# The tail of a relu-and-mean kernel: another cut of the last row, a third partial sum, and another order of the last three waits

## The chip, the cores and the metric

The kernel runs on one core of a Trainium2 chip. The metric is device time in microseconds (us), lower is better. A span is the time of one profiled execution as its trace has it; it is about 1.3 us shorter than the device time of the same run.

## The reference

```python
x: (32, 512, 1024) float32
return np.mean(np.maximum(x, 0), axis=-1)      # (32, 512) float32
```

That is 16384 rows of 1024 numbers: 67.1 MB in, 64 KB out, and one pass of cheap arithmetic.

## The kernel before

All rows are streamed from HBM (the memory that holds x) into SBUF (the memory that the engines compute from) by DMA loads that SyncE issues. Two compute engines, ScalarE and VectorE, take the rows by turns, each with one instruction that applies the maximum with 0 and adds up along the row. The loads grow smaller toward the end (16 rows a partition, then 6, 4, 2, 1), and the last row of each partition comes in three pieces of columns, so that little work is left after the last byte. Each load and each engine raises a semaphore, a counter that others wait for; an engine's count below is the update that says that its piece of the last row is done. In the code P is 128 partitions and D 1024 columns, and the comments are added for this text.

```python
col_pieces = [512, 256, 256]
...
last = sbuf("last", P, D + 2)            # the last row, and 2 columns for partial sums
scale = sbuf("scale", P, D // 4 + 2)     # 1/1024 everywhere
...
nc.scalar.wait_ge(loaded[i + 1], 16)     # first piece
act_row(nc, last[:, :512], last[:, D:D + 1]).then_inc(act, 1)
nc.vector.wait_ge(loaded[i + 2], 16)     # second piece
dve_row(nc, last[:, 512:768], last[:, D + 1:D + 2]).then_inc(dve, 1)
nc.vector.wait_ge(act, n_done + 1)       # ScalarE's count: its partial sum is there
nc.vector.wait_ge(dve, n_done + 1)       # VectorE's own count: its own partial sum is there
nc.vector.wait_ge(loaded[i + 3], 16)     # third piece
nc.vector.scalar_tensor_tensor(          # the last instruction: third piece and both partial sums
    out=last[:, 768:], in0=last[:, 768:], scalar=0.0, in1=scale[:, :],
    op0=ALU.max, op1=ALU.mult, accum_out=res[:, J - 1:J],
).then_inc(dve, 1)
... # SyncE waits for it and stores res
```

The last instruction reads 256 columns and the two partial sums behind them in one go. The source makes it wait for three things. In the program as it is built, each compute instruction carries at most one wait. The one that the source writes first goes on the instruction itself, and the two others go on one EventSemaphore instruction ahead of it (called the wait instruction from here on). So here the wait instruction carries the load and the own count, and the last instruction itself waits for ScalarE's count.

Of the kernel before, what the change touches and what calls it, by code (L numbers as in the profile page):

```python
# [12 lines left out]
def act_row(nc, src, acc):  # L13

    return nc.scalar.activation(out=src, in_=src, func=ACT.Relu, accum_out=acc)  # L15


def dve_row(nc, src, acc, init=None):

    return nc.vector.tensor_scalar(  # L20
        out=src, in0=src, scalar1=0.0, scalar2=init,
        op0=ALU.max, op1=ALU.add, accum_out=acc,
    )
# [22 lines left out]
def kernel(  # L46
# [10 lines left out]
    nc = tc.nc  # L57
    P = nc.NUM_PARTITIONS
    xf = x.flatten_outer_dims()
    R, D = xf.shape  # L60
# [13 lines left out]

    row_pieces = [6, 4, 2, 1]
    assert full * NB + sum(row_pieces) + 1 == J
    col_pieces = [512, 256, 256]
    assert sum(col_pieces) == D

    def sbuf(name, *shape):  # L80
        return ctx.enter_context(nc.sbuf_tensor(name, list(shape), F32))
# [2 lines left out]
    sums, res, part = sbuf("sums", P, J), sbuf("res", P, J), sbuf("part", P, 2)  # L84


    last = sbuf("last", P, D + 2)
    scale = sbuf("scale", P, D // 4 + 2)

    row0, mean0, turned0 = sbuf("row0", P, 2, D), sbuf("mean0", P, 32), sbuf("turned0", P, 32)  # L90

# [1 line left out]
    loaded = [nc.alloc_semaphore(f"loaded{i}") for i in range(full + len(row_pieces) + len(col_pieces) + 2)]  # L93
    act, dve, pool = (nc.alloc_semaphore(n) for n in ("act", "dve", "pool"))
# [38 lines left out]
    lo, i = 0, full  # L133
    for n in row_pieces:
        load(i, xt[:, lo:lo + n, :], xr[:, j0 + lo:j0 + lo + n, :])
        lo, i = lo + n, i + 1
    c = 0
    for w in col_pieces:
        load(i, last[:, c:c + w], xr[:, J - 1, c:c + w])
        c, i = c + w, i + 1  # L140
# [37 lines left out]
    lo, i = 0, full  # L178
    for n in row_pieces[:-1]:
        rows(i, xt, lo, n, j0)  # L180
        lo, i = lo + n, i + 1
# [12 lines left out]
        out=res[:, J - 2:J - 1], in0=part[:, 0:1], scalar1=part[:, 1:2], scalar2=inv, op0=ALU.add, op1=ALU.mult,  # L194
    ).then_inc(pool, 1)
    nc.scalar.wait_ge(loaded[i + 1], 16)
    act_row(nc, last[:, :512], last[:, D:D + 1]).then_inc(act, 1)
    nc.vector.wait_ge(loaded[i + 2], 16)
    dve_row(nc, last[:, 512:768], last[:, D + 1:D + 2]).then_inc(dve, 1)
    nc.vector.wait_ge(act, n_done + 1)  # L200
    nc.vector.wait_ge(dve, n_done + 1)
    nc.vector.wait_ge(loaded[i + 3], 16)
    nc.vector.scalar_tensor_tensor(  # L203
        out=last[:, 768:], in0=last[:, 768:], scalar=0.0, in1=scale[:, :], op0=ALU.max, op1=ALU.mult,
        accum_out=res[:, J - 1:J],
# [51 lines left out]
```

## Time and profile before

| | before |
|---|---|
| device time, median of 6 runs | 161.22 us (161.08 to 161.26) |
| span of the profiled run | 159.8 us |
| DMA queue, share of 16 engines' time | 97.8% |
| VectorE, ScalarE busy | 46%, 44% |
| last row's three pieces completely landed | 156.936, 157.298, 157.604 us |
| last VectorE instruction starts | 157.839 us |

The first four rows are read from the results and from the head of the page. The last two come from the trace's records of semaphore updates and instructions, which have single nanoseconds; the views round to 10 ns. The DMA engines carry the kernel and the compute engines wait for them (VectorE 84.6 us and ScalarE 83.8 us for main loads, by the view of waits). Only the two microseconds after the stream (157.604 to 159.795) are open to a change like this one. The prediction shows the lines.

### The profile page before, as it was taken

How to read it: one execution, taken by the hardware profiler on the slowest of the kernel's cores; microseconds unless marked ns; L12 is line 12 of the kernel's file. 1: busy time of each engine (PE TensorE's matmuls, PEld its weight loads, DVE VectorE, ACT ScalarE, POOL GpSimd, SP SyncE). 2: the span in 40 equal slices, each digit the busy share in tenths (PEclk: the TensorE clock that was granted, in tenths of full speed). 3: DMA queues.
4: the chain of work that ended last, by engine and by line, in shares of the span. 5: the costliest groups of instructions: out<-in, count | busy, mean ns of one | idle time of the engine just before them, and what ended most of it. 6: DMA issues, size and time to landing. Idle time of an engine off the chain costs nothing. (4 is left out here: it accounts for less than half of the span.)

```text
span 159.8 us, 350 instructions
## 1 busy us (share of the span) xinstructions
DVE 73.1 (46%) x131; ACT 70.3 (44%) x133; POOL 1.3 (1%) x9
## 2 busy tenths in 40 slices
DVE  0000029900499002990049800597007950089995
ACT  1400029800499002980049600595007930089974
POOL 1000000000000000000000000000000000000001
DMA  9969979899996997998979979969969969899993
GB/s 394 525 262 525 476 312 525 377 410 525 394 509 279 525 476 312 525 410 377 525 345 443 525 312 476 525 262 525 525 262 525 525 262 525 355 400 427 416 407 112
DMA packets 2608, 67.18 MB, mean 420 GB/s; under 512 B 560, under 2 KB 816, under 8 KB 1328
## 3 DMA queue, kind: packets, MB, share of 16 engines
q1 hardware_dynamic: 2608, 67.18, 97.8%
HBM read 67.11 MB, written 0.07 MB: 420 GB/s over the span
## 5 line engine op out<-in xcount | busy, mean ns | idle before, releaser
L20 DVE TENSOR_SCALAR_CACHE_REDUCE rows<-rows 128x1024 f32<-128x1024 f32 (+1 forms) x63 | 71.9, 1208 | 84.6 <-DMA rows<-in_x_dram 84.6
L15 ACT ACTIVATE rows<-rows 128x1024 f32<-128x1024 f32 (+1 forms) x63 | 65.2, 1035 | 83.9 <-DMA rows<-in_x_dram 83.8
L15 ACT ACTIVATION_READ_ACCUMULATOR rows<-rows 128x1 f32 x63 | 11.7, 186 | 0.0
L20 DVE DVE_READ_ACCUMULATOR rows<-rows 128x1 f32 x63 | 5.2, 82 | 0.0
L169 ACT ACT_TABLE_LOAD x1 | 1.3, 1283 | 3.5 <-DMA row<-in_x_dram 3.5
L169 ACT ACTIVATE row<-row 128x1024 f32<-128x1024 f32 x2 | 2.1, 1047 | 0.0
L159 POOL TENSOR_SCALAR res<-sums 128x112 f32<-128x112 f32 (+1 forms) x2 | 0.5, 244 | 153.9 <-DVE rows L20 153.9
L15 ACT ACTIVATE last<-last 128x512 f32<-128x512 f32 x1 | 0.6, 629 | 0.0
L20 DVE TENSOR_SCALAR_CACHE_REDUCE last<-last 128x256 f32<-128x256 f32 x1 | 0.4, 419 | 0.3 <-DMA last<-in_x_dram 0.3
L203 DVE SCALAR_TENSOR_TENSOR last<-last,scale 128x258 f32<-128x258 f32 x1 | 0.4, 428 | 0.1
L169 ACT ACTIVATION_READ_ACCUMULATOR row<-row 128x1 f32 x2 | 0.4, 186 | 0.0
L175 DVE STREAM_TRANSPOSE turned<-mean 128x32 f32<-128x32 f32 x1 | 0.2, 211 | 0.3 <-ACT row L169 0.3
L144 POOL MEMSET scale<- 128x258 f32 x1 | 0.3, 313 | 0.0
L193 POOL TENSOR_SCALAR res<-part 128x1 f32<-128x1 f32 x1 | 0.3, 264 | 0.5 <-DVE rows L20 0.5
L15 ACT ACTIVATION_READ_ACCUMULATOR last<-last 128x1 f32 x1 | 0.2, 186 | 0.0
L143 POOL MEMSET mean<- 128x32 f32 x1 | 0.1, 124 | 1.5 <-POOLq L55 1.5
L241 POOL MEMSET const-bfloat16-1.0<- 128x1 bf16 x1 | 0.1, 102 | 0.0
L241 POOL MEMSET const-uint8-127<- 128x1 uint8 x1 | 0.1, 102 | 0.0
L241 POOL MEMSET const-float32-0.0<- 128x1 f32 x1 | 0.1, 99 | 0.2 <-issue 0.2
L241 POOL MEMSET const-float32-1.0<- 128x1 f32 x1 | 0.1, 99 | 0.0
L203 DVE DVE_READ_ACCUMULATOR last<-last,scale 128x1 f32 x1 | 0.1, 85 | 0.0
L20 DVE DVE_READ_ACCUMULATOR last<-last 128x1 f32 x1 | 0.1, 82 | 0.0
## 6 DMA issues: line engine op xcount, KB each, us to landing
rows<-in_x_dram SPq DMA_DIRECT2D x1, 3072.0 KB, 36.7
rows<-in_x_dram SPq DMA_DIRECT2D x1, 2048.0 KB, 41.2
row<-in_x_dram SPq DMA_DIRECT2D x2, 512.0 KB, 22.3
rows<-in_x_dram SPq DMA_DIRECT2D x1, 1024.0 KB, 43.2
rows<-in_x_dram SPq DMA_DIRECT2D x1, 512.0 KB, 44.1
last<-in_x_dram SPq DMA_DIRECT2D x1, 256.0 KB, 44.3
last<-in_x_dram SPq DMA_DIRECT2D x2, 128.0 KB, 44.0
rows<-in_x_dram SPq DMA_DIRECT2D x7, 48.8
```

The lines of the kernel that those rows point to most:

```text
L15: return nc.scalar.activation(out=src, in_=src, func=ACT.Relu, accum_out=acc)
L20: return nc.vector.tensor_scalar(out=src, in0=src, scalar1=0.0, scalar2=init, op0=ALU.max, op1=ALU.add, accum_out=acc,)
L143: nc.gpsimd.memset(mean0[:, :], 0.0)
L144: nc.gpsimd.memset(scale[:, :], inv).then_inc(pool, 1)
L159: nc.gpsimd.tensor_scalar(out=res[:, lo:hi], in0=sums[:, lo:hi], scalar1=inv, scalar2=0.0, op0=ALU.mult, op1=ALU.add,).then_inc(pool, 1)
L169: done = nc.scalar.activation(out=row0[:, c, :], in_=row0[:, c, :], func=ACT.Relu, scale=inv, accum_out=mean0[:, c:c + 1],)
L175: nc.vector.transpose(turned0[:, :], mean0[:, :]).then_inc(first, 1)
L193: nc.gpsimd.tensor_scalar(out=res[:, J - 2:J - 1], in0=part[:, 0:1], scalar1=part[:, 1:2], scalar2=inv, op0=ALU.add, op1=ALU.mult,).then_i ...
L203: nc.vector.scalar_tensor_tensor(out=last[:, 768:], in0=last[:, 768:], scalar=0.0, in1=scale[:, :], op0=ALU.max, op1=ALU.mult, accum_out=r ...
L241: nc = _bacc.Bacc("TRN2", target_bir_lowering=False, num_devices=1)
```

## The change

The intent is to have less VectorE work after the last pieces land. The border between first and second piece moves from column 512 to 576. VectorE uses the time in which it is idle (0.29 us ahead of its piece in the trace of before) to take 128 columns of the first piece (a third partial sum), ScalarE keeps 448, and VectorE's second piece shrinks from 256 to 192 columns. The source also writes the load's wait ahead of the two counts, so that the last VectorE instruction itself waits for the last load.

```diff
-    col_pieces = [512, 256, 256]
+    col_pieces = [576, 192, 256]
...
-    last = sbuf("last", P, D + 2)
-    scale = sbuf("scale", P, D // 4 + 2)
+    last = sbuf("last", P, D + 3)
+    scale = sbuf("scale", P, D // 4 + 3)
...
     nc.scalar.wait_ge(loaded[i + 1], 16)
-    act_row(nc, last[:, :512], last[:, D:D + 1]).then_inc(act, 1)
+    act_row(nc, last[:, :448], last[:, D:D + 1]).then_inc(act, 1)
+    nc.vector.wait_ge(loaded[i + 1], 16)
+    dve_row(nc, last[:, 448:576], last[:, D + 1:D + 2])
     nc.vector.wait_ge(loaded[i + 2], 16)
-    dve_row(nc, last[:, 512:768], last[:, D + 1:D + 2]).then_inc(dve, 1)
+    dve_row(nc, last[:, 576:768], last[:, D + 2:D + 3]).then_inc(dve, 1)
+    nc.vector.wait_ge(loaded[i + 3], 16)
     nc.vector.wait_ge(act, n_done + 1)
     nc.vector.wait_ge(dve, n_done + 1)
-    nc.vector.wait_ge(loaded[i + 3], 16)
```

By the rule above, the wait instruction now carries the own count and ScalarE's count, and the last instruction itself waits for the load.

## The prediction

> **What bounds the kernel now.** I read the page's head and its 40 slices first, then the chain of waits, then the timeline of the last 10 us, and at the end the trace's own records of instructions and semaphore updates. These have single nanoseconds, and they also hold the wait instructions, which no view prints.
>
> ```profile
> span 159.8 us, 350 instructions
> DVE 73.1 (46%) x131; ACT 70.3 (44%) x133; POOL 1.3 (1%) x9
> DMA  9969979899996997998979979969969969899993
> q1 hardware_dynamic: 2608, 67.18, 97.8%
> ```
>
> Neither compute engine is busy half of the time and the DMA engines are full until the last slice. 67.18 MB have to come in, and the change moves not one byte of that. So what the change can touch is the stretch after the stream: from the landing of the last row's pieces to the final store. The timeline shows that stretch (start, duration, engine, line, operation, shapes):
>
> ```profile
> 156.27 0.58 ACT L15 ACTIVATE rows<-rows 128x448 f32<-128x448 f32 x1
> 156.27 0.75 DVE L20 TENSOR_SCALAR_CACHE_REDUCE rows<-rows 128x576 f32<-128x576 f32 x1
> 156.76 0.19 ACT L15 ACTIVATION_READ_ACCUMULATOR rows<-rows 128x1 f32 x1
> 156.95 0.08 DVE L20 DVE_READ_ACCUMULATOR rows<-rows 128x1 f32 x1
> 156.96 0.63 ACT L15 ACTIVATE last<-last 128x512 f32<-128x512 f32 x1
> 157.32 0.42 DVE L20 TENSOR_SCALAR_CACHE_REDUCE last<-last 128x256 f32<-128x256 f32 x1 [0.29 <-DMA last<-in_x_dram]
> 157.50 0.19 ACT L15 ACTIVATION_READ_ACCUMULATOR last<-last 128x1 f32 x1
> 157.67 0.08 DVE L20 DVE_READ_ACCUMULATOR last<-last 128x1 f32 x1
> 157.84 0.43 DVE L203 SCALAR_TENSOR_TENSOR last<-last,scale 128x258 f32<-128x258 f32 x1
> 158.19 0.09 DVE L203 DVE_READ_ACCUMULATOR last<-last,scale 128x1 f32 x1
> 158.30 0.34 SPq L214 DMA_DIRECT2D out_dram<-res  x1
> ```
>
> The reader should see two things. VectorE stands idle for 0.29 us before its 256-column piece, and a DMA ended that idle time. Then the last instruction, at 157.84, starts 0.17 us after the accumulator read at 157.67, where rows of the main loop follow each other without such a gap. The chain of waits says the same of the end:
>
> ```profile
> 157.75 0.09 issue
> 157.84 0.12 DVE last L203
> ```
>
> From here on everything is fixed cost: the last instruction takes from 157.84 to 158.29, the store is issued at 158.30, and its landing at 159.80 is the end of the span. **Time gained or lost at the start of the last instruction is time of the whole kernel, one for one.**
>
> Which of its three waits ended last? The records of semaphore updates say so. The three pieces have landed completely at 156.936, 157.298 and 157.604. ScalarE's count goes up at 157.691 and VectorE's own count, for the 256-column piece, at 157.760. The wait instruction before the last one ends at 157.795 and the last one starts at 157.839. So the last wait is VectorE's own partial sum (157.760), then ScalarE's, 0.069 us earlier, then the load, 0.156 us earlier. The path is: second piece lands 157.298, reduction starts 157.321, accumulator read 157.666, count 157.760, wait over 157.795, last instruction 157.839.
>
> [...] one stands on VectorE from 157.632 to 157.795. Built from the source, the kernel before has the load and VectorE's own count on it, and ScalarE's count on the last instruction; the program puts on the instruction itself the wait that the source writes first. The change writes the load first, so the load goes on the instruction and the two counts on the EventSemaphore. [...] from a reduction's start to its accumulator read it took 678 ns for 576 columns and 345 ns for 256, so 1.04 ns a column and 79 ns fixed[...]. [...] In the trace the first piece's sixteen come from 156.466 to 156.936[...].
>
> **The change part by part.**
>
> Loads. The order and the total are the same, so the second and third piece should land as before, at 157.298 and 157.604. Only the border of the first moves. A packet of 2048 bytes takes 85 ns at the median and one of 1024 bytes 46 ns, so 256 bytes more cost 10 ns. There are 128 packets on 16 engines, 8 each, so the 576-column piece lands 8 x 10 = 0.08 us later: 157.015. From the landings (1024 bytes took 157.298 - 156.936 = 0.362 us) it would be 0.09; I choose 0.08.
>
> ScalarE. It loses 64 columns (448 for 512) but starts later. It was ready at 156.95, just as its piece landed, so every nanosecond of the later landing counts. Its start is 157.015 + 0.023 = 157.038. The row piece of the same 448 columns gives the duration: 484 ns from its start to its accumulator read, then 195 ns to the count (157.496 to 157.691 in the last row). The count goes up at 157.038 + 0.484 + 0.195 = 157.717. Before it was 157.691, so ScalarE is **0.026 us later, in spite of less work**.
>
> VectorE, the added piece. 128 columns take 79 + 128 x 1.04 = 212 ns to the accumulator read. It starts with ScalarE at 157.038 and leaves the engine at 157.250, inside the 0.29 us of idle time, before the second piece lands at 157.298. It costs nothing on the path.
>
> VectorE, the second piece. 192 columns for 256 is 64 x 1.04 = 67 ns less. It starts at 157.321 as before, reads its accumulator at 157.600, and the count goes up 94 ns later, at 157.694. Before it was 157.760: 0.066 us earlier.
>
> The last instruction. The EventSemaphore now ends with the later of 157.694 and 157.717. **That is ScalarE, and it takes 0.023 us of the 0.066 back.** The net gain is 157.760 - 157.717 = 0.043 us. With the same 79 ns from count to start, the last instruction starts at 157.796, shown as 157.80. The move of the load's wait onto the instruction is worth nothing, as the load is there 0.11 us before the later count. The third partial sum makes its operands 259 wide in place of 258: 1 ns.
>
> Sum: 0.04 us off a median of 161.19 gives **161.15 us**, and a span of 159.75 or 159.76.
>
> **The rivals.** (a) *ScalarE does not hold it back.* If the larger piece lands less than 0.06 us later, VectorE's count is the last and the whole 0.066 us come: 161.12. [...] Against it: the stream is full up to there. (b) *The new small pieces hold VectorE.* If the 128-column piece, its accumulator read and the next wait take more than the idle time, the second reduction starts late. From 157.250 to 157.321 there are 0.07 us in hand; a delay of 0.15 us would eat that and the gain, and the time would stay at 161.19 or go to 161.25. For it: two reductions with a wait between them, which the trace of before doesn't have at this size. Against it: in the main loop the next reduction starts with the accumulator read, not after it. (c) *The load is what matters*, as the change's wording suggests. If in most executions the third piece lands after 157.76 (in this profile 157.604), the wait on the instruction itself saves the step from wait instruction to instruction, the 44 ns from 157.795 to 157.839, but the shorter sums save nothing: again about 161.15, by another road. Against it: it would have to land 0.16 us later. (d) *The last piece lands later* because of packets of 768 and 2304 bytes: up to 0.1 us slower, 161.29. Nothing in the trace shows a cost beyond bytes for these sizes, as packets of 1024 and 2048 bytes differ nearly by their bytes.
>
> **Range and chances.** All four lie between 161.1 and 161.3, closer together than I can tell from three runs, which spread from 161.08 to 161.24. The mechanism is worth 0.03% and the spread 0.1%; the range is the spread of single runs and a little for another session: 160.95 to 161.35. For 2% it would have to move by 3.2 us, more than all that lies between the last landing (157.604) and the end of the span; only a disturbed stream could do that. Faster 0.01, same 0.98, slower 0.01.
>
> **What would show each step.** In the timeline after: ScalarE's 448-column piece of the last row starts at about 157.04 and not 156.96; a 128-column reduction starts with it; the 192-column reduction starts at 157.32, its idle time down from 0.29 to below 0.1; its accumulator read is at 157.60 and ScalarE's at 157.52; the last instruction starts at 157.80, and the store is issued at 158.26. In the semaphore records ScalarE's count is the later one. Since each trace has its own jitter in the stream, the distances from the second landing (before: 0.541 us to the last instruction's start; after, expected: 0.498) say more than the absolute times. I am wrong on the mechanism if VectorE's count is the later one, if the 192-column reduction starts over 0.05 us after its piece has landed, or if the last landing releases the last instruction. I am wrong on the time if it leaves the range, which would mean that the stream itself moved.

The 79 ns fixed and 1.04 ns a column of a reduction were read from the trace of before. "One" is the wait instruction ahead of the last instruction, and the "sixteen" are the updates of the first piece's semaphore; ScalarE started on that piece at 156.959, 23 ns after the last of them. That the 128 packets of a piece fall 8 to an engine is the author's estimate (128 over 16 engines), not shown.

## The result, and the profile after

| | before | after |
|---|---|---|
| median of 6 runs each | 161.22 us (161.08 to 161.26) | 161.19 us (161.13 to 161.37) |
| ratio, 95% interval | | 1.0002 (0.9989 to 1.0014) |
| span of the profiled run | 159.8 us | 159.9 us |
| pieces landed | 156.936, 157.298, 157.604 | 157.114, 157.390, 157.682 |
| ScalarE's count, VectorE's own count | 157.691, 157.760 | 157.815, 157.786 |
| last instruction starts | 157.839 | 157.908 |

A ratio is the mean time of one kernel's fast runs over that of the other's fast runs of the same rounds, so it is not quite the ratio of the medians. The two kernels are the same within 0.15%, as predicted. The changed kernel's trace is even 0.07 us longer. The head of its page shows the same limit as before:

```profile
span 159.9 us, 352 instructions
DVE 73.3 (46%) x133; ACT 70.2 (44%) x133; POOL 1.3 (1%) x9
DMA  9969979989996996997999979969969969899993
```

Two instructions more on VectorE (the 128-column reduction and its accumulator read), and the DMA engines full until the last slice. The timeline of the tail (start, duration, engine, line, operation, shapes) answers to the one in the prediction:

```profile
157.03 0.08 DVE L20 DVE_READ_ACCUMULATOR rows<-rows 128x1 f32 x1
157.14 0.58 ACT L15 ACTIVATE last<-last 128x448 f32<-128x448 f32 x1
157.14 0.29 DVE L20 TENSOR_SCALAR_CACHE_REDUCE last<-last 128x128 f32<-128x128 f32 x1
157.35 0.08 DVE L20 DVE_READ_ACCUMULATOR last<-last 128x1 f32 x1
157.41 0.35 DVE L20 TENSOR_SCALAR_CACHE_REDUCE last<-last 128x192 f32<-128x192 f32 x1
157.62 0.19 ACT L15 ACTIVATION_READ_ACCUMULATOR last<-last 128x1 f32 x1
157.69 0.08 DVE L20 DVE_READ_ACCUMULATOR last<-last 128x1 f32 x1
157.91 0.43 DVE L205 SCALAR_TENSOR_TENSOR last<-last,scale 128x259 f32<-128x259 f32 x1
158.26 0.08 DVE L205 DVE_READ_ACCUMULATOR last<-last,scale 128x1 f32 x1
158.37 0.34 SPq L216 DMA_DIRECT2D out_dram<-res  x1
```

The 128-column reduction lies in what was idle time, and the 192-column one starts at once when its piece is there (landed 157.390, started 157.413). That is as intended. But look at the distance from VectorE's accumulator read to the last instruction: 157.67 to 157.84 before, 157.69 to 157.91 now. It has grown from 0.17 to 0.22 us. The chain of waits (start, duration, what) gives a reason:

```profile
157.62 0.20 ACT last L15
157.81 0.05 DVEq L204
157.86 0.04 issue
157.91 0.12 DVE last L205
```

It names ScalarE's accumulator read, then the wait instruction (DVEq L204), then the last instruction. Read alone, this confirms the prediction's story that ScalarE's later count holds the end back. The experiments show that this reading is wrong.

**Where the 0.07 us of the two spans come from.** They are the stream's, not the change's. The loads are already later by about 0.09 us when the first main load lands (22.871 before, 22.963 after), and still so at the third (62.852 before, 62.947 after), 50 us before the first changed load is issued. The expectations below count from zero and call the third one the second. To be free of this, the experiments measure **d, the time from the complete landing of the second piece to the start of the last instruction**. It is 0.541 us before and 0.518 us after; the prediction expected 0.498. What follows the last instruction's start is nearly fixed: to the last landing of the store it took 1.922 to 1.933 us in all twelve traces.

### The profile page after: what moved, and what is told of

It is laid out like the page before. It is cut to its first block, busy times and chain, and to the rows that moved or that the text cites. A ratio compares the mean times of both kernels' runs of the same rounds, so it can differ in the third digit from the quotient of the medians.

```text
span 159.9 us, 352 instructions
## 1 busy us (share of the span) xinstructions
DVE 73.3 (46%) x133; ACT 70.2 (44%) x133; POOL 1.3 (1%) x9
## 2 busy tenths in 40 slices
DMA packets 2608, 67.18 MB, mean 420 GB/s; under 512 B 560, under 2 KB 816, under 8 KB 1328
## 3 DMA queue, kind: packets, MB, share of 16 engines
q1 hardware_dynamic: 2608, 67.18, 97.8%
HBM read 67.11 MB, written 0.07 MB: 420 GB/s over the span
## 4 chain that ended last, share of the span: by engine, by line
DMA 73%; DVE 17%; another core or an unknown queue 6%; SPq 1%; issue 1%; ACT 0%; DVEq 0%
DMA rows<-in_x_dram 45%; DMA last<-in_x_dram 28%; DVE rows L20 17%; SPq L109 1%; ACT last L15 0%; DVE last L205 0%; DVEq L204 0%; SPq L115 0%; DVEq L148 0%
## 5 line engine op out<-in xcount | busy, mean ns | idle before, releaser
L20 DVE TENSOR_SCALAR_CACHE_REDUCE last<-last 128x128 f32<-128x128 f32 (+1 forms) x2 | 0.6, 320 | 0.0
L15 ACT ACTIVATE last<-last 128x448 f32<-128x448 f32 x1 | 0.6, 577 | 0.1
```

The costliest lines, as they stand in the source:

```text
L15: return nc.scalar.activation(out=src, in_=src, func=ACT.Relu, accum_out=acc)
L20: return nc.vector.tensor_scalar(out=src, in0=src, scalar1=0.0, scalar2=init, op0=ALU.max, op1=ALU.add, accum_out=acc,)
```

## The experiments

All ten runs gave correct results. Terms used: a count is in place at the time of its semaphore update. "Own" is VectorE's own count.

### after_again and before_again: both kernels once more

No edit. The question is how far two traces of one kernel differ, and whether the change shifts the stream.

> The changed kernel once more, for a second trace. Measure used in all runs: distance d from the complete landing of the last row's second piece to the start of the last VectorE instruction (kernel before 0.541 us, changed kernel 0.518 us). Theory (the later count, here ScalarE's, starts the last instruction): d 0.50 to 0.54, ScalarE's count after VectorE's by 0.01 to 0.05 us, time within 0.15 us of the kernel before. Rival (the change shifts the whole stream by 0.08 us, as the first pair of traces has it from the first load on): the second main load lands again 0.09 us later than before's 62.85 us and the span is again 159.87 us or more.

> The kernel before once more, for a second trace. If the 0.08 us by which the stream came later in the changed kernel's trace is scatter of the stream, this trace's second main load lands anywhere from 62.80 to 62.97 us; if the change causes it, at 62.85 again within 0.02. d again 0.541 within 0.02 us, VectorE's own count the last.

Measured: d = 0.519 and 0.543, so d repeats within 2 ns. The third main load landed at 62.751 in the changed kernel's second trace and at 62.877 in that of before: the order has turned round, so the shift is scatter of the stream and the rival falls. (before_again's 62.877 alone would hardly have parted the two. Over all twelve traces the mean is 62.84 us with the old pieces and 62.83 with the new.) The end of the ramp (the landing of the load ahead of the last row) lay anywhere from 156.071 to 156.326 in the twelve traces, 0.26 us, ten times what the change gains in d. Timed beside the kernel before: 161.03 us for 161.15 (ratio 0.9994, 0.9982 to 1.0007), and 161.13 for 161.15 (0.9999, 0.9985 to 1.0013). The time cannot resolve the change; d can.

### order_only: the kernel before, with the order of the waits alone changed

```diff
+    nc.vector.wait_ge(loaded[i + 3], 16)
     nc.vector.wait_ge(act, n_done + 1)
     nc.vector.wait_ge(dve, n_done + 1)
-    nc.vector.wait_ge(loaded[i + 3], 16)
```

> The kernel before with the order of the three waits alone changed. Theory: the load is there 0.15 us before the own count, so moving its wait onto the instruction gives nothing: d stays 0.54 within 0.02 us. Rival (the wait on the instruction itself is what gains): d falls by 0.04 us or more, to 0.50 or less.

Measured: d = 0.584, which neither theory had: 0.042 us **longer** than the mean of the two traces of before (0.542). The counts had not moved (own 0.463, ScalarE's 0.395 us after the second landing). The step from the own count to the start of the last instruction grew from 79 to 121 ns. The chain of waits shows where:

```profile
157.30 0.44 DVE last L20 x2
157.74 0.03 issue
157.77 0.05 DVEq L202
157.82 0.04 issue
157.86 0.12 DVE last L203
```

From the own count (157.739) 28 ns pass until the wait instruction starts, 49 ns until it is over, 44 ns until the last instruction starts. In the kernel before, the wait instruction started at 157.632, which is 28 ns after the load that it carries first, and was over 35 ns after the own count that it carries second. So a wait instruction seems to start with its first condition and then to need about 50 ns at least, even when the second condition has long been met, as here. Time: 161.25 us for 161.15 (ratio 1.0014, 0.9998 to 1.0029), the same.

### own_count: the kernel before, with the own count on the last instruction

```diff
-    nc.vector.wait_ge(act, n_done + 1)
     nc.vector.wait_ge(dve, n_done + 1)
+    nc.vector.wait_ge(act, n_done + 1)
     nc.vector.wait_ge(loaded[i + 3], 16)
```

> The kernel before, with VectorE's own count (the wait that ends last there) as the one that the last instruction itself waits for, and ScalarE's count and the load on the wait instruction. If it matters which wait stands on the instruction, the step from own count to start falls from 79 ns to about 25 (as from a landing to a reduction's start, 23 ns), and d falls to 0.49 us. If that step is a fixed cost of a wait on the own result, it stays 79 ns and d stays 0.54. Time: a gain of 0.05 us is inside the scatter; within 0.15 us of the kernel before under both.

Measured: d = 0.486, as the first theory said. The own count came at 157.722 and the last instruction started at 157.745, 23 ns later. No wait instruction is left in the chain:

```profile
157.28 0.44 DVE last L20 x2
157.72 0.02 issue
157.75 0.11 DVE last L203
```

One moved line gained 0.057 us in d against the second trace of before on the same chip (0.543), more than twice what the whole change gained. Time: 161.04 us for 161.15, ratio 1.0005 (0.9987 to 1.0024).

These runs gave **theory W**: the start of the last instruction is the latest of three times, namely the condition on the instruction itself plus 23 ns, the one second on the wait instruction plus 79 ns, and the one first there plus 122 ns. It says of the changed kernel: own count 0.396 + 0.122 = 0.518, ScalarE's count 0.425 + 0.079 = 0.504. Then the own count in its bad place decides there, not ScalarE. The prediction's theory S says that ScalarE's count decides. The trace of the changed kernel alone doesn't part them, because its two counts lie 29 ns apart: with the step of 79 ns that was measured before, S would give d = 0.504, and it reaches the measured 0.518 if the step is taken as 93. The next four runs part them.

### pieces_only: the changed kernel with the wait order of before

```diff
-    nc.vector.wait_ge(loaded[i + 3], 16)
     nc.vector.wait_ge(act, n_done + 1)
     nc.vector.wait_ge(dve, n_done + 1)
+    nc.vector.wait_ge(loaded[i + 3], 16)
```

> The changed kernel with the wait order of the kernel before: the load and the own count on the wait instruction (the own count named second), ScalarE's count on the last instruction. Theory W, from the first four runs: a count on the instruction itself starts it 23 ns later, one named second on the wait instruction 79 ns later, one named first there 121 to 123 ns later, and the latest of the three decides. With the changed kernel's counts (VectorE's 0.396, ScalarE's 0.425 us after the second landing) W gives d = 0.475 (own count 0.396 + 0.079). If the new order of the waits cost nothing, d stays 0.518.

Measured: d = 0.476. Without the new wait order the new pieces gain 0.065 us over before (0.541), close to the 66 ns by which the own count came earlier (0.462 to 0.396); the new order takes 0.042 of it back. Time: 161.19 us for 161.17, ratio 1.0005 (0.999 to 1.002).

### act_384: the changed kernel with 64 columns fewer for ScalarE

```diff
-    act_row(nc, last[:, :448], last[:, D:D + 1]).then_inc(act, 1)
+    act_row(nc, last[:, :384], last[:, D:D + 1]).then_inc(act, 1)
     nc.vector.wait_ge(loaded[i + 1], 16)
-    dve_row(nc, last[:, 448:576], last[:, D + 1:D + 2])
+    dve_row(nc, last[:, 384:576], last[:, D + 1:D + 2])
```

> The changed kernel with ScalarE taking 384 of the first piece's columns, VectorE 192. ScalarE's count comes about 53 ns earlier (0.372 us after the second landing), VectorE's stays at 0.396. Theory S (the prediction's: ScalarE's later count holds the last instruction back): d falls to 0.475. Theory W: the own count is named first on the wait instruction and costs 122 ns, so d stays at 0.518, and the wait instruction still takes about 50 ns though both counts are there.

Measured: ScalarE's count came at 0.373, now ahead of the own count at 0.395, and d stayed at 0.518. This is W's number to the nanosecond and 0.043 us away from S's. The chain of waits no longer names ScalarE, yet the wait instruction takes the same 0.05 us:

```profile
156.92 0.65 DVE last L20 x4
157.57 0.03 issue
157.60 0.05 DVEq L204
157.65 0.04 issue
157.69 0.12 DVE last L205
```

So **ScalarE's later count did not hold back the changed kernel**, though its chain of waits named it. Time: 161.04 us for 161.17, ratio 0.9992 (0.9978 to 1.0006).

### before_swapped and after_swapped: only the two counts change places

In before_swapped the load is written first, then the own count, then ScalarE's; it differs from order_only in the order of the two counts alone. In after_swapped the same two lines of the changed kernel change places.

```diff
     nc.vector.wait_ge(loaded[i + 3], 16)
-    nc.vector.wait_ge(act, n_done + 1)
     nc.vector.wait_ge(dve, n_done + 1)
+    nc.vector.wait_ge(act, n_done + 1)
```

> The kernel before with the load on the instruction, ScalarE's count first and the own count second on the wait instruction; against order_only only those two change places. W: d falls from order_only's 0.584 back to 0.541, step 79 ns. If it is the load's wait on the instruction that cost 42 ns in order_only, d stays 0.584.

> The changed kernel with the same two counts in the other order: ScalarE's first, the own count second. W: ScalarE's count at 0.425 plus 121 ns, d = 0.546, slower than the changed kernel by 28 ns. If the later count decides and the order between the two is nothing (S): d stays 0.518.

Measured: 0.543 in before_swapped (W: 0.541, the rival: 0.584) and 0.551 in after_swapped (W: 0.546, S: 0.518). The same swap makes one kernel 41 ns quicker and the other 33 ns slower, because another count is the late one. It is therefore not the load on the last instruction that costs, but a late count in the first place of the wait instruction. Times: 161.09 us for 161.17 (0.9995, 0.9981 to 1.001) and 161.05 for 161.17 (0.9991, 0.9977 to 1.0006). The kernel with the longer d has the lower median of the two, which shows once more what these times cannot tell.

### pieces_own and act_384_own: the best that W suggests

The changed kernel with the own count on the last instruction, and ScalarE's count second; act_384_own also has the edit of act_384.

```diff
-    nc.vector.wait_ge(loaded[i + 3], 16)
-    nc.vector.wait_ge(act, n_done + 1)
     nc.vector.wait_ge(dve, n_done + 1)
+    nc.vector.wait_ge(act, n_done + 1)
+    nc.vector.wait_ge(loaded[i + 3], 16)
```

> The changed kernel with VectorE's own count on the last instruction, the load first and ScalarE's count second on the wait instruction. W: own count 0.395 + 0.023 = 0.418, ScalarE's count 0.425 + 0.079 = 0.504, load about 0.31 + 0.121 = 0.43; the latest gives d = 0.504. Here, and only with this order, ScalarE is what holds the last instruction. If the two instructions' own order didn't matter, d would be 0.518 as in the changed kernel.

> As pieces_own, with ScalarE taking 384 columns of the first piece and VectorE 192. W: ScalarE's count 0.373 + 0.079 = 0.452, own count 0.418, load about 0.43 to 0.44; d = 0.452, the shortest of all, 0.09 us under the kernel before and 0.067 under the changed kernel. The same edit (384 for 448) that moved d by nothing in act_384 then moves it by 0.05 us here. The time would fall by 0.09 us, 0.06%, inside the scatter of the timed runs: within 0.15 us of the kernel before.

Measured: d = 0.492 and 0.432. Both are shorter than expected, by 12 and 20 ns, because the counts themselves came at other times than assumed, not because the rule failed. In pieces_own the third piece landed late, 0.370 us after the second, so the load, first on the wait instruction, decided: 0.370 + 0.122 = 0.492. By the same rule ScalarE's count would have allowed a start 8 ns sooner (0.405 + 0.079 = 0.484). So the expectation that ScalarE would be seen to decide there is a miss. (The chain of waits of this trace names ScalarE all the same; that the load decided follows from the rule and was not tested by a run of its own.) In act_384_own ScalarE's count came at 0.353, and 0.353 + 0.079 = 0.432. With d = 0.432, act_384_own has the shortest tail of all twelve traces, 0.109 us under the kernel before and 0.086 under the changed kernel. In time this is not to be seen: 161.08 us for 161.20 (ratio 0.9998, 0.9982 to 1.0015), and for pieces_own 161.04 for 161.20 (0.9997, 0.9982 to 1.0011).

### All twelve traces

The times are nanoseconds after the landing of the second piece. The order is that on the wait instruction (first, second), then what the last instruction itself waits for: L load, A ScalarE's count, D own count. W is the latest of first + 122, second + 79, itself + 23.

| trace | order | D | A | L | W | d |
|---|---|---|---|---|---|---|
| before | L D, A | 462 | 393 | 306 | 541 | 541 |
| before_again | L D, A | 463 | 384 | 307 | 542 | 543 |
| after | D A, L | 396 | 425 | 292 | 518 | 518 |
| after_again | D A, L | 396 | 426 | 337 | 518 | 519 |
| order_only | D A, L | 463 | 395 | 325 | 585 | 584 |
| own_count | L A, D | 463 | 395 | 298 | 486 | 486 |
| pieces_only | L D, A | 396 | 411 | 303 | 475 | 476 |
| act_384 | D A, L | 395 | 373 | 321 | 517 | 518 |
| before_swapped | A D, L | 463 | 394 | 323 | 542 | 543 |
| after_swapped | A D, L | 396 | 428 | 289 | 550 | 551 |
| pieces_own | L A, D | 396 | 405 | 370 | 492 | 492 |
| act_384_own | L A, D | 396 | 353 | 291 | 432 | 432 |

The three constants were read from the first six traces. With each trace's own counts they give the last six to 1 ns, without a new fit. By this rule the first place decides in six traces (with D, A and L in it), the second in five (D and A), the place on the instruction itself in own_count alone. The wait instruction's own record shows where the constants come from: in all twelve it started 27 to 28 ns after its first condition, and was over at the later of 49 to 50 ns after its start and 35 ns after its second condition. Except in own_count, where the last instruction's own condition came later, that instruction started 44 to 45 ns after that: 28 + 50 + 44 = 122 and 35 + 44 = 79.

Seen from VectorE's own accumulator read, the last instruction started 117 ns later with the own count's wait on the instruction (94 to the count and 23 from there; own_count), 173 ns later with it second on the wait instruction (before), and 217 ns later with it first there (changed kernel). No run left this wait out, so what it costs as such, and whether the result needs it, is not shown. Reductions of the main loop, which have no wait between them, start with the accumulator read before them (both at 150.55 in the trace of before).

## Why the prediction was right or wrong

**The time was right:** 161.15 predicted, 161.19 measured, and the range held both medians of the changed kernel (161.19, 161.03), though two of its single runs lay just above it (161.37, 161.36). The reason for "same" was right as well. The DMA stream bounds the kernel (97.8% of the engines' time in both pages), the change moves no byte, and the tail offers some hundredths of a microsecond against a scatter of 0.1% and more. But the right time says nothing for the mechanism: the range held all four rivals as well, and no time here can tell 0.02 us from 0.04.

**Small misreadings, without effect on the sum.** The 67.18 MB are all that the queue moved, with the stores; 67.11 MB came in. The end of the span is not the store's landing (159.761 in the trace) but the end of SyncE's wait for it, at 159.795.

**Loads: right in kind, a little too small.** The larger first piece was expected to land 0.08 us later, by the estimate of 8 packets an engine. Its distance from the landing of the load before it was 0.662 to 0.696 us in the five traces with 512 columns (mean 0.683) and 0.769 to 0.788 in the seven with 576 (mean 0.779): 0.095 us. The prediction's other estimate, 0.09 from the spacing of the landings, was the better one. The second piece was expected not to move; from the same load it came on average 1.061 us for 1.045, 16 ns later. Single traces scatter by 35 ns, so this last difference is suggested, not settled. If it is real, it takes most of the 23 ns that the changed kernel gains in d.

**VectorE's work: right.** The 128-column reduction took 211 ns to its accumulator read (predicted 212) and fitted into the idle time. The own count came 0.396 us after the second landing, for 0.462: the 66 ns that were predicted.

**ScalarE: the count was right, its effect was wrong.** Its count came after the own one by 29 ns (predicted 23). But the step "The EventSemaphore now ends with the later of 157.694 and 157.717. That is ScalarE, and it takes 0.023 us of the 0.066 back" fails. act_384 brings ScalarE's count forward by 52 ns and d does not move.

**The wait order: the step that failed.** The prediction said "With the same 79 ns from count to start" and "The move of the load's wait onto the instruction is worth nothing". It costs 42 ns, shown by order_only on the old pieces (0.584 against 0.542, the mean of the two traces of before) and by pieces_only on the new ones (0.476 against 0.518). Moving the load away from the wait instruction pushes the own count from second to first place there, where the same count costs about 122 ns in place of 79. So the sum of the change is: shorter VectorE sum -66 ns, worse place of the own count +43 ns, together -23 ns in d (measured 0.541 to 0.518). The prediction got -43 ns from -66 and +23. It had a right size for VectorE and a wrong term beside it. By luck the wrong term has the same sign as the right one, and the chain of waits of the changed kernel names ScalarE, so the story looked confirmed.

**The rivals and the signs.** (b) and (d) fell: the second reduction started 23 ns after its piece, and the third piece landed on average 0.315 us after the second in the seven traces with the new pieces, for 0.312 in the five with the old. (a), that ScalarE does not hold it back, was right in its wording but not in its reason or its number: the larger piece landed 0.095 us later, not less than 0.06, ScalarE's count was the later one, and the wait order took the gain. (c) fell: the load was there 104 ns before the own count. None of the signs named as proof against the mechanism appeared, and it was wrong all the same. The signs asked which condition came last and whether the second reduction started late, and none asked how long the step from that count to the start was. Only that the start came 0.02 us later than predicted, relative to the landing, betrayed it. **Still open** is how the wait instruction works inside. That it takes its conditions one after the other, in the order of the built program, fits all twelve traces to 1 ns, but it is inferred from start and end times. That a place costs the same whatever condition stands in it is shown for the first place with all three conditions, and for the second with the two counts; the place on the instruction itself decided in own_count alone.

## What to carry to other kernels

When the last instruction of a chain waits for several things, put the one that comes last in the trace on the instruction itself and the next latest in second place on the wait instruction. This is shown for one VectorE instruction with a wait instruction of two conditions. In this kernel the place alone was worth up to 0.1 us for one count (23, 79 or 122 ns), which can be seen in a trace and in none of the times measured here. A chain of waits that names the latest count does not prove that this count decides: bring it forward and see whether the end moves, and measure from the nearest event that the change doesn't touch, since the stream ahead of it scattered here ten times as far as the gain.
